# Attention's scores in one PSUM tile, scores and products tied in urgent chains

## The chip, the cores and the metric

The kernel runs on one core of a Trainium2 chip. The metric is the time of one execution in device microseconds; the time before is 1723.08 us, the median of three runs (1722.53 to 1729.99).

## The reference

Two request groups of 512 tokens with 1024 features pass through two layers with shared weights. Layer 0 is a bidirectional RWKV-7 time mixing with two scans; layer 1, which the change touches, is a neighbourhood attention over a grid of 8 rows x 64 columns with 16 heads of 64 features:

```python
proj = xn @ w_in + b_in
q, k, v, z = jnp.split(proj, 4, axis=-1)
...
s = jnp.einsum('bnqhd,bsnkhd->bhnqsk', qr, kr, preferred_element_type=f32)
s = jnp.where(mask, s + bias.astype(f32), NEG_INF)
p = jax.nn.softmax(s.reshape(s.shape[:4] + (-1,)), axis=-1).reshape(s.shape)
return jnp.einsum('bhnqsk,bsnkhd->bnqhd', p.astype(v.dtype), vr)
...
return (o.reshape(bsz, t, D_INNER) * jax.nn.silu(z)) @ w_o + b_o
```

Each token attends to a window of 8 rows x 16 columns. Norms stand before and after each layer.

## The kernel before, in words

Features lie on partitions, tokens on the free axis. A projection (`gemm`, L398 to L409) fills one PSUM bank of 128x512 with 24 matmuls: eight steps over the features, each as three matmuls of operands split in a high and a low part (L404 to L406). Its weights come by DMA through `raw`, are cast by ACT (L353, `whi`) and subtracted by DVE (L354, `wlo`).

The scan of layer 0 runs under an order written by hand. Behind it, `rest()` (L1655) opens new PSUM banks: two `pg` for projections, two `pt` for transposed probabilities, one `po` for attention's output, three `pm` for everything else. From here a scheduler orders each engine's queue: it takes the instruction with the lowest priority number among those that its own clock holds ready, and numbers run in program order. `high_priority(n)` lowers the numbers by n; `behind` (L263) makes one instruction stand behind another on one engine, without a semaphore. Engines then run their queues strictly in this order.

`rest()` weaves generators. The first request's last in-projections (`inproj`, L1298, four projections q, k, v, z for each pair of heads) and the out-projection of layer 0 (`out0`) are run with steps of attention (`heads`) between; then come the first request's output projection (`out1`, L1394), the norm in the second request (`norm0`, `rstds`: a sum by matmuls at L430, ACT and DVE, then a spread to all partitions by matmuls at L442), the second request's in-projections with its `heads`, transposes of the residual (`by_token`, L1421), and at last `last()` (L1427), the second request's output projection (L1463 to L1465). `inproj` evacuates on DVE (L1311) and ACT (L1315 to L1323) and stores q, k, v and z to DRAM (L306); `heads` loads them (L309).

`heads(s, p)` does a pair of heads. v is transposed by PE in two groups of four and three (L1342, in `pm`), copied by ACT to `vtok` (L1343). Then two rounds of two windows each follow. A round has four score matmuls (L1353), two windows n for each of two heads h; head 0 works on partitions 0 to 63, head 1 on 64 to 127, and each head has its `pm` tile. DVE adds the bias and takes the maximum (L1361), ACT takes the exponential (L1364), DVE divides (L1365, L1366), PE transposes two blocks for each score (L1368, in `pt`), and ACT copies them to `pts` (L1371). Eight product matmuls with v (L1381, two windows, two blocks e, two heads) add into `po`, with 64 output columns for each head. DVE multiplies `po` by the gate z (L1387). With 16 pairs of heads there are 32 rounds.

The words for matmul forms in the profile are rows*columns of the array: 128*128 for projections and transposes, 64*128 for scores, 128*64 for products. The prediction calls the latter two split forms, and one uninterrupted run of scores or of products on PE's queue a visit.

Of the kernel before, what the change touches and what calls it, by code (L numbers as in the profile page):

```python
# [13 lines left out]
ALU = mybir.AluOpType  # L14
# [4 lines left out]
P = 128  # L19
# [194 lines left out]
class Trunk:  # L214
    NACT, NW, NRAW, NXR, NTMP, WP = 18, 4, 3, 3, 5, 512
    POST0, POST, POST2, POST3, NPA = 0.7, 1.0, 0.15, 0.66, 5
    HP, HS = (1000, 0), 1000
    OUT1 = ("pg", "pg", "pm", "pm")
    LOW = 15
    LA = -40  # L220
    LATER = (0, 40, 0, 0)
    POST4 = 0.2
    LAST = ("pg", "pg", "pm", "pm")
    PG, PT, NK, NPT = 2, 2, 2, 3
# [1103 lines left out]
    def heads(self, s, p):  # L1328

        nc = self.nc  # L1330
        vt, act, gps = nc.vector, nc.scalar, nc.gpsimd
        a = lambda tag, shape=(P, T), n=1, dt=F32: self.t(tag, shape, n, dt, self.ap)
        bias = a("bias", (P, 2, 3, 256), self.NBI)
        for h in range(2):
            self.load(bias[:, h].rearrange("p a b -> p (a b)"), self.a["rpb"][2 * p + h])
        q, k, v = (self.load(a(kind, n=2), self.sp[kind, s, p]) for kind in ("q1", "k1", "v1"))
        yield
        vtok = a("vtok", (P, 7, P), self.NK)
# [6 lines left out]
        op = self.p("po", (P, 4, P))  # L1345
        cols = (0, 8, 24, 32)
        for ns in ((0, 1), (2, 3)):

            scs = [self.p("pm", (P, 2, 256)) for h in range(2)]
            for n in ns:  # L1350
                for h in range(2):
                    hs = slice(64 * h, 64 * h + 64)
                    nc.tensor.matmul(  # L1353
                        scs[h][:, n % 2], q[hs, n * P:(n + 1) * P], k[hs, 8 * cols[n]:8 * cols[n] + 256], start=True, stop=True)
            pts = []
            for n in ns:
                pt = self.p("pt", (P, 2, 2, P))
                for h in range(2):
                    sb = a("sb", (P, 256), self.NSB)
                    mx = a("mx", (P, 4), 6)  # L1360
                    vt.tensor_tensor_reduce(  # L1361
                        sb, scs[h][:, n % 2], bias[:, h, (0, 1, 1, 2)[n]], 1.0, -3.0e38, op0=ALU.add, op1=ALU.max, accum_out=mx[:, 0:1])
                    vt.tensor_scalar(mx[:, 1:2], mx[:, 0:1], -1.0, None, op0=ALU.mult)  # L1363
# [10 lines left out]
            if ns[1] == 3:  # L1374
                while ("z1", s, p) not in self.sp:
                    yield
                z = self.load(a("z1"), self.sp["z1", s, p])
            for n in ns:
                for e in range(2):
                    for h in range(2):  # L1380
                        nc.tensor.matmul(  # L1381
                            op[64 * h:64 * h + 64, n], vtok[:, cols[n] // 8 + 2 * e, 64 * h:64 * h + 64], pts[n % 2][:, h, e],
                            start=(e == 0), stop=(e == 1))
            yield
# [270 lines left out]
    def rest(self, prep, mid):  # L1655
        prep.close()
        mid.close()
        self.banks(self.stack, pg=self.PG, pt=self.PT, po=1, pm=7 - self.PG - self.PT)
        self.gt = "pg"
# [165 lines left out]
```

## Time and profile before

| what | us |
|---|---|
| median of three runs | 1723.08 |
| profiled execution, its own time | 1721.11 |
| its span, first to last instruction | 1719.3 |
| PE busy in the span | 1583.5 |
| DVE busy | 1246.5 |
| ACT busy | 982.9 |
| first matmul of `rest()` starts at | 1178.81 |

Read the page's slices first, to see in which part of the span an engine is full; then cut that part out in the table by windows; then read the timeline by start times. Matmuls overlap on PE, so the distance from one start to the next is what one costs, and the duration in its row is longer.

### The profile page before, as it was taken

Reading aid. Unit: us, or ns where it says so; the run is one execution under the profiler, and the core shown is the slowest. Engines: PE = TensorE matmul, PEld = TensorE weight load, DVE = VectorE, ACT = ScalarE, POOL = GpSimd, SP = SyncE. Lnnn points to the kernel's source line nnn. Section 1 sums busy time; section 2 is a strip of 40 time slices with the busy share of each in tenths; the row PEclk is TensorE's granted clock in tenths of the full one; section 3 lists DMA queues with packets and bytes.
Section 4 is the critical chain, followed back from the end, with each engine's and each line's share of the span. In section 5 each row is a group of like instructions: output and inputs, shape, how many; then the busy total and the mean of one; then the engine's idle time right before and its main releaser. Section 6 shows DMA issues by size and latency. Waiting matters only on the chain. (4 is left out here: it accounts for less than half of the span.)

```text
span 1719.3 us, 45887 instructions
## 1 busy us (share of the span) xinstructions
PE 1583.5 (92%) x18624; PEld 1209.3 (70%) x18624; DVE 1246.5 (73%) x2725; ACT 982.9 (57%) x1975; POOL 24.1 (1%) x94
## 2 busy tenths in 40 slices
PE   7999787999988999789988799999999999999998
PEld 6766555776766767567766677777777787777776
DVE  8986678788877867898788898655565586555474
ACT  5444655767755675656576545544556664555462
POOL 0000000000000000000000000000000000000000
PEclk9989999999999989899999799999999999999999
DMA  5435687786566678766587564547564248555553
GB/s 204 166 117 202 208 278 230 221 273 224 184 201 205 206 239 252 240 217 216 188 263 229 191 209 146 177 147 246 178 197 146 93 147 268 163 164 160 163 169 98
DMA packets 240819, 336.23 MB, mean 196 GB/s; under 512 B 53696, under 2 KB 119360, under 8 KB 240608
## 3 DMA queue, kind: packets, MB, share of 16 engines
q1 hardware_dynamic: 240608, 333.31, 60.4%
q8 instruction: 146, 2.39, 0.6%
q14 instruction: 65, 0.53, 0.1%
HBM read 227.71 MB, written 105.51 MB: 194 GB/s over the span
## 5 line engine op out<-in xcount | busy, mean ns | idle before, releaser
L747 PE MATMUL pm<-act,whi 128*128 128x512 f32 x608 | 272.9, 449 | 13.1 <-ACT whi L699 9.9
L749 PE MATMUL pm<-act,wlo 128*128 128x512 f32 x608 | 248.8, 409 | 18.2 <-DVE wlo L701 18.2
L748 PE MATMUL pm<-act,whi 128*128 128x512 f32 x608 | 248.9, 409 | 7.7 <-DVE act L727 6.1
L404 PE MATMUL pg<-act,whi 128*128 128x512 f32 x448 | 181.4, 406 | 0.0
L405 PE MATMUL pg<-act,whi 128*128 128x512 f32 x448 | 178.1, 398 | 0.0
L406 PE MATMUL pg<-act,wlo 128*128 128x512 f32 x448 | 178.0, 398 | 0.0
L353 ACT CAST whi<-raw 128x512 fp32r<-128x512 f32 x156 | 96.2, 617 | 142.6 <-PE pg L405 71.8
L354 DVE TENSOR_TENSOR wlo<-raw,whi 128x512 fp32r<-128x512 f32 x156 | 106.7, 686 | 73.9 <-ACT whi L353 56.9
L747 PEld LDWEIGHTS pm<-act,whi 128*128 128x128 f32 x608 | 119.3, 196 | 56.3 <-issue 13.9
L749 PEld LDWEIGHTS pm<-act,wlo 128*128 128x128 f32 x608 | 119.9, 197 | 52.1 <-DVE wlo L701 25.4
L748 PEld LDWEIGHTS pm<-act,whi 128*128 128x128 f32 x608 | 120.1, 198 | 30.5 <-DVE act L727 8.6
L701 DVE TENSOR_TENSOR wlo<-raw,whi 128x512 fp32r<-128x512 f32 x152 | 102.8, 683 | 33.3 <-ACT whi L699 32.6
L699 ACT CAST whi<-raw 128x512 fp32r<-128x512 f32 x152 | 92.7, 617 | 27.9 <-PE pm L748 11.1
L404 PEld LDWEIGHTS pg<-act,whi 128*128 128x128 f32 x448 | 84.2, 188 | 23.7 <-issue 8.8
L406 PEld LDWEIGHTS pg<-act,wlo 128*128 128x128 f32 x448 | 84.2, 188 | 18.9 <-issue 2.8
L405 PEld LDWEIGHTS pg<-act,whi 128*128 128x128 f32 x448 | 84.3, 188 | 17.8 <-issue 3.0
L938 DVE TENSOR_TENSOR N<-etmp,N 128x30 f32<-128x30 f32 (+14 forms) x240 | 79.8, 332 | 8.3
L1361 DVE CUSTOM_DVE_ANT_0 sb<-pm,bias 128x256 f32<-128x256 f32 x128 | 50.1, 420 | 47.3 <-PE pm L1353 36.1
L937 DVE TENSOR_TENSOR etmp<-N 128x30 f32<-128x30 f32 (+14 forms) x240 | 78.7, 328 | 4.8
L1364 ACT ACTIVATE sb<-sb,mx 128x256 f32<-128x256 f32 x128 | 64.1, 502 | 30.7 <-DVE mx L1363 30.5
L1022 PE MATMUL pf<-cab 64*64 64x128 f32 (+1 forms) x2048 | 72.4, 270 | 3.4 <-issue 2.4
L1045 DVE TENSOR_TENSOR AK<-zy,cc 128x256 f32<-128x256 f32 x63 | 26.6, 422 | 64.2 <-PE zy L1010 64.0
(363 smaller groups left out, 3379.1 us busy)
## 6 DMA issues: line engine op xcount, KB each, us to landing
dab<-ab SPq DMA_DIRECT2D x32, 1024.0 KB, 7.1
cab<-dab SPq DMA_DIRECT2D x64, 512.0 KB, 4.5
raw<-in_w_in_dram SPq DMA_DIRECT2D x128, 256.0 KB, 2.9
bias<-in_rpb_dram SPq DMA_DIRECT2D x32, 384.0 KB, 4.7
raw<-in_w_z_dram SPq DMA_DIRECT2D x32, 256.0 KB, 4.6
dz<-tmp SPq DMA_DIRECT2D x32, 256.0 KB, 2.2
raw<-in_w_k_dram SPq DMA_DIRECT2D x32, 256.0 KB, 2.5
dk<-tmp SPq DMA_DIRECT2D x32, 256.0 KB, 3.0
```

What stands on the lines that cost most here:

```text
L353: self.nc.scalar.copy(hi, src)
L354: (eng or self.nc.vector).tensor_tensor(lo, src, hi.bitcast(F32), op=ALU.subtract)
L404: nc.tensor.matmul(ps, hi, x[k][0], start=(k == 0), stop=False)
L405: nc.tensor.matmul(ps, hi, x[k][1], start=False, stop=False)
L406: nc.tensor.matmul(ps, lo, x[k][0], start=False, stop=(k == KT - 1))
L699: nc.scalar.copy(hi, raw[h])
L701: nc.vector.tensor_tensor(lo, raw.pop(h), hi.bitcast(F32), op=ALU.subtract)
L747: nc.tensor.matmul(ps, hi[:, at], xh, start=(k == 0), stop=False)
L748: nc.tensor.matmul(ps, hi[:, at], xl, start=False, stop=False)
L749: nc.tensor.matmul(ps, lo[:, at], xh, start=False, stop=(k == KT - 1))
L937: vt.tensor_tensor(tv, N[:, q + 1:, q:q + 1].broadcast_to([P, n, q]), N[:, q:q + 1, :q].broadcast_to([P, n, q]), op=ALU.mult)
L938: vt.tensor_tensor(N[:, q + 1:, :q], tv, N[:, q + 1:, :q], op=ALU.add)
```

## The change

The four scores of a round share one tile `sc` of two banks, a bank for each head, with one buffer; `pm` keeps one bank (the sum stays eight). The scores of a round get the priority 1000 ahead and each stands behind the one before, so that they come in the order window 0 head 0, window 0 head 1, window 1 head 0, window 1 head 1. The products with v get the same, with the round's second window first. `out1` takes `pg` for all eight projections; `last()` takes `po` for its third bank. Line numbers from 219 on are one higher in the changed kernel, from the scores on three to eleven higher.

```diff
--- before.py
+++ after.py
@@ -215,12 +215,13 @@
     NACT, NW, NRAW, NXR, NTMP, WP = 18, 4, 3, 3, 5, 512
     POST0, POST, POST2, POST3, NPA = 0.7, 1.0, 0.15, 0.66, 5
     HP, HS = (1000, 0), 1000
-    OUT1 = ("pg", "pg", "pm", "pm")
+    OUT1 = ("pg", "pg", "pg", "pg")
+    HPA = 1000
     LOW = 15
     LA = -40
     LATER = (0, 40, 0, 0)
     POST4 = 0.2
-    LAST = ("pg", "pg", "pm", "pm")
+    LAST = ("pg", "pg", "po", "pm")
     PG, PT, NK, NPT = 2, 2, 2, 3
     AHEAD, AHEADW, SCAN_A, SCAN_W = 0, 0, 300, 300
     NAB, NX, NR, NY, NSB, NBI = 2, 2, 2, 2, 4, 1
@@ -1346,12 +1347,17 @@
         cols = (0, 8, 24, 32)
         for ns in ((0, 1), (2, 3)):
 
-            scs = [self.p("pm", (P, 2, 256)) for h in range(2)]
-            for n in ns:
-                for h in range(2):
-                    hs = slice(64 * h, 64 * h + 64)
-                    nc.tensor.matmul(
-                        scs[h][:, n % 2], q[hs, n * P:(n + 1) * P], k[hs, 8 * cols[n]:8 * cols[n] + 256], start=True, stop=True)
+            scs = self.p("sc", (P, 2, 2, 256))
+            with self.tc.high_priority(self.HPA):
+                last = None
+                for n in ns:
+                    for h in range(2):
+                        hs = slice(64 * h, 64 * h + 64)
+                        one = nc.tensor.matmul(
+                            scs[:, h, n % 2], q[hs, n * P:(n + 1) * P], k[hs, 8 * cols[n]:8 * cols[n] + 256], start=True, stop=True)
+                        if last is not None:
+                            self.behind(one, last)
+                        last = one
             pts = []
             for n in ns:
                 pt = self.p("pt", (P, 2, 2, P))
@@ -1359,7 +1365,7 @@
                     sb = a("sb", (P, 256), self.NSB)
                     mx = a("mx", (P, 4), 6)
                     vt.tensor_tensor_reduce(
-                        sb, scs[h][:, n % 2], bias[:, h, (0, 1, 1, 2)[n]], 1.0, -3.0e38, op0=ALU.add, op1=ALU.max, accum_out=mx[:, 0:1])
+                        sb, scs[:, h, n % 2], bias[:, h, (0, 1, 1, 2)[n]], 1.0, -3.0e38, op0=ALU.add, op1=ALU.max, accum_out=mx[:, 0:1])
                     vt.tensor_scalar(mx[:, 1:2], mx[:, 0:1], -1.0, None, op0=ALU.mult)
                     act.activation(sb, sb, AF.Exp, bias=mx[:, 1:2], accum_out=mx[:, 2:3])
                     vt.reciprocal(mx[:, 3:4], mx[:, 2:3])
@@ -1375,12 +1381,17 @@
                 while ("z1", s, p) not in self.sp:
                     yield
                 z = self.load(a("z1"), self.sp["z1", s, p])
-            for n in ns:
-                for e in range(2):
-                    for h in range(2):
-                        nc.tensor.matmul(
-                            op[64 * h:64 * h + 64, n], vtok[:, cols[n] // 8 + 2 * e, 64 * h:64 * h + 64], pts[n % 2][:, h, e],
-                            start=(e == 0), stop=(e == 1))
+            with self.tc.high_priority(self.HPA):
+                last = None
+                for n in ns[::-1]:
+                    for e in range(2):
+                        for h in range(2):
+                            one = nc.tensor.matmul(
+                                op[64 * h:64 * h + 64, n], vtok[:, cols[n] // 8 + 2 * e, 64 * h:64 * h + 64], pts[n % 2][:, h, e],
+                                start=(e == 0), stop=(e == 1))
+                            if last is not None:
+                                self.behind(one, last)
+                            last = one
             yield
         with self.tc.high_priority(self.HP[s] if p == NP - 1 else 0):
             o = self.tmp() if s else self.t("oa", (P, T), NP, F32, self.ap)
@@ -1655,7 +1666,7 @@
     def rest(self, prep, mid):
         prep.close()
         mid.close()
-        self.banks(self.stack, pg=self.PG, pt=self.PT, po=1, pm=7 - self.PG - self.PT)
+        self.banks(self.stack, pg=self.PG, pt=self.PT, po=1, sc=1, pm=5 - self.PG - self.PT)
         self.gt = "pg"
         self.ap = self.pool(self.stack)
         queue = [self.heads(0, p) for p in range(self.NPA)]
```

The first place is on PE, at the first pair of heads (`sc`, and before `pm` from 16341 up, are scores; `pt` transposed probabilities; other `pm` with v are v's transposes; `pg` is a projection). Before, an x2 of one tile is two windows of one head:

```order
L404 MATMUL pg_16389<-act_13337,whi_16385 128x512
L1353 MATMUL pm_16342<-k_2857_16312,q_2856_16310 128x256 x2
L1353 MATMUL pm_16442<-k_2857_16312,q_2856_16310 128x256 x2
L405 MATMUL pg_16389<-act_13336,whi_16385 128x512
L406 MATMUL pg_16389<-act_13337,wlo_16386 128x512
L404 MATMUL pg_16487<-act_12216,whi_16479 128x512
L1368 MATMUL pt_16347<-cc,sb_16348 128x128 x2
L405 MATMUL pg_16487<-act_12215,whi_16479 128x512
L406 MATMUL pg_16487<-act_12216,wlo_16480 128x512
```

The same place in the change:

```order
L406 MATMUL pg_16391<-act_13336,whi_16387 128x512
L1343 MATMUL pm_16335<-cc,v_2859_16317 128x128 x2
L1356 MATMUL sc_16444<-k_2858_16315,q_2857_16313 128x256 x4
L1343 MATMUL pm_16335<-cc,v_2859_16317 128x128
L1374 MATMUL pt_16349<-cc,sb_16350 128x128 x2
L1374 MATMUL pt_16349<-cc,sb_16370 128x128 x2
L1374 MATMUL pt_16403<-cc,sb_16404 128x128 x2
L1374 MATMUL pt_16403<-cc,sb_16416 128x128 x2
L407 MATMUL pg_16391<-act_13337,wlo_16388 128x512
```

The second round's scores stood as head 0 beside the first round's head 1, and its head 1 came later; now the four are one row, and the first round's eight transposes stand together.

The second place is on PE too, at the second pair of heads, whose second round has the tiles 16706 and 16707:

```order
L406 MATMUL pg_16658<-act_12970,wlo_16655 128x512
L1353 MATMUL pm_16706<-k_2922_16573,q_2921_16571 128x256
L1353 MATMUL pm_16707<-k_2922_16573,q_2921_16571 128x256
L1368 MATMUL pt_16608<-cc,sb_16624 128x128 x2
L1368 MATMUL pt_16665<-cc,sb_16666 128x128 x2
L1353 MATMUL pm_16706<-k_2922_16573,q_2921_16571 128x256
L1368 MATMUL pt_16665<-cc,sb_16678 128x128 x2
L1353 MATMUL pm_16707<-k_2922_16573,q_2921_16571 128x256
L404 MATMUL pg_16658<-act_13286,whi_16654 128x512
```

In the change this round's scores are `sc_16706`, and `po_16343` is the first pair's output:

```order
L406 MATMUL pg_16565<-act_12560,whi_16561 128x512
L407 MATMUL pg_16565<-act_12561,wlo_16562 128x512
L1389 MATMUL po_16343<-pts_16528,vtok_16322 64x128 x4
L1389 MATMUL po_16343<-pts_16495,vtok_16322 64x128 x4
L1356 MATMUL sc_16706<-k_2921_16574,q_2920_16572 128x256 x4
L1343 MATMUL pm_16594<-cc,v_2922_16576 128x128 x3
L1374 MATMUL pt_16608<-cc,sb_16609 128x128 x2
L405 MATMUL pg_16565<-act_12970,whi_16561 128x512
L406 MATMUL pg_16565<-act_12969,whi_16561 128x512
```

Scores that stood in four rows among transposes are one row, directly behind the first pair's last eight products.

The third place is the last norm of the first request on PE (sum L430, spread L442). Before, the spread stands 18 projection matmuls behind the sum:

```order
L406 MATMUL pg_18861<-act_18747,wlo_18854 128x512
L430 MATMUL pm_18817<-ones,acc_3375_18320 128x1 x4
L404 MATMUL pg_18861<-act_18751,whi_18853 128x512
L405 MATMUL pg_18861<-act_18750,whi_18853 128x512
L406 MATMUL pg_18861<-act_18751,wlo_18854 128x512
L404 MATMUL pg_18861<-act_18755,whi_18853 128x512
```

In the change (sum L431, spread L443, with one `pm` bank):

```order
L406 MATMUL pg_18848<-act_18757,whi_18844 128x512
L407 MATMUL pg_18848<-act_18758,wlo_18845 128x512
L431 MATMUL pm_18804<-ones,acc_3360_18307 128x1 x4
L443 MATMUL pm_18817<-tmp_18812,ones 128x128 x4
L405 MATMUL pg_18913<-act_18730,whi_18905 128x512
L406 MATMUL pg_18913<-act_18729,whi_18905 128x512
```

The spread is now the sum's direct neighbour, and the next projection stands behind both.

## The prediction

> **What bounds the kernel now.** I read the page first: its slices for where in the span PE is full, then the chain that ended last.
>
> ```profile
> PE   7999787999988999789988799999999999999998
> ...
> PE 36%; DVE 4%; DMA 2%; ACT 2%; issue 1%; SPq 0%; DVEq 0%; ACTq 0%
> PE pg L404 6%; PE pg L405 6%; PE pg L406 6%; PE pm L1353 3%; PE po L1381 2%; PE pt L1368 2%; PE pm L747 2%; PE pm L748 1%; PE pm L749 1%; DMA raw<-in_w_ao_dram 1%; DMA raw<-in_w_in_dram 1%; PE pf L1022 1%; PE pm L1342 1%; PE us L1119 1%; PE zy L1093 0%
> ```
>
> The last slices are full on PE, and the chain runs mostly through PE: the projections (L404 to L406), then scores, products and transpositions of attention. All the edits lie in this last stage, from the first matmul of `rest()` to PE's last one. So I cut that stretch out in the table by windows, and asked what PE waited for there:
>
> ```profile
> 1178.80:1711.50 532.70, 529.75 (x2849) 408.38 (x2847) 316.76 (x971) 293.65 (x649) 0.00 (x0) 1.00 0.52 166
> ...
> PE pm L1342 <- DMA v<-dv: 2.2, 1, 2.2
> PE pm L1353 <- ACT vtok L1343: 0.4, 1, 0.4
> PE pg L1463 <- ACT os L353: 0.3, 1, 0.3
> ```
>
> The columns of the first row are length, PE, PEld, DVE, ACT. PE is busy 529.75 of 532.70 us and waits 2.9 us in all; DVE is busy 59%, ACT 55%. The granted clock is 1.00. The stage is as long as PE's queue of matmuls, so the change is worth what it does to that queue, less the waits it adds. "Busy" doesn't yet say that the array is used well: the start times do.
>
> **What an attention visit costs PE.** These rows of the timeline show start, time and form; a score or a product is listed as two matmuls, so x8 under L1353 is four scores, x4 two.
>
> ```profile
> 1196.25 0.39 PE L405 MATMUL pg<-act,whi 128*128 128x512 f32 x1
> 1196.47 0.39 PE L406 MATMUL pg<-act,wlo 128*128 128x512 f32 x1
> 1196.79 1.13 PE L1353 MATMUL pm<-k,q 64*128 64x256 f32 x4
> 1197.85 0.50 PE L404 MATMUL pg<-act,whi 128*128 128x512 f32 x1
> 1198.19 0.40 PE L405 MATMUL pg<-act,whi 128*128 128x512 f32 x1
> ...
> 1216.79 0.70 PE L1353 MATMUL pm<-k,q 64*128 64x256 f32 x4
> 1217.42 0.66 PE L1368 MATMUL pt<-cc,sb 128*128 128x128 f32 x4
> ...
> 1516.07 1.13 PE L1353 MATMUL pm<-k,q 64*128 64x256 f32 x8
> 1517.14 0.50 PE L404 MATMUL pg<-act,whi 128*128 128x512 f32 x1
> ...
> 1230.08 0.60 PE L1342 MATMUL pm<-cc,v 128*128 128x128 f32 x4
> 1230.43 0.48 PE L404 MATMUL pg<-act,whi 128*128 128x512 f32 x1
> 1230.84 0.66 PE L1381 MATMUL po<-pts,vtok 128*64 128x128 f32 x8
> 1231.43 0.50 PE L405 MATMUL pg<-act,whi 128*128 128x512 f32 x1
> ...
> 1212.10 1.09 PE L1381 MATMUL po<-pts,vtok 128*64 128x128 f32 x16
> 1213.12 0.50 PE L405 MATMUL pg<-act,whi 128*128 128x512 f32 x1
> ...
> 1274.55 0.66 PE L1381 MATMUL po<-pts,vtok 128*64 128x128 f32 x8
> 1275.14 0.66 PE L1368 MATMUL pt<-cc,sb 128*128 128x128 f32 x4
> 1275.55 0.48 PE L405 MATMUL pg<-act,whi 128*128 128x512 f32 x1
> ```
>
> Projection matmuls start 0.22 to 0.23 apart; I use 0.227. What follows from start to start:
> - Two scores of one head (at 1196.79; the order shows one tile) hold PE 1.06 us. Four scores, two of each head (1516.07), hold it 1.07. Two scores of different heads (1216.79) hold it 0.63. The heads run side by side; the price goes by the head with most scores: 0.63 for one, 1.06 for two, 0.43 more for each further.
> - Products of one window (1230.84) hold PE 0.59, of both windows of a round (1212.10) 1.02.
> - Entering such a split form takes 0.32 instead of 0.227 (1196.47 to 1196.79): 0.09 more. Leaving it to projections takes 0.34 for the first (1197.85 to 1198.19): 0.11 more. Leaving to transpositions takes 0.06 more: 0.41 for four after a product (1275.14) against 0.35 after a projection (1230.08).
>
> **The change, part by part.** Only the order and the waits change; all matmuls stay. I counted the visits in both orders on PE, from the first score to the end.
>
> *Scores in one tile, tied.* Before: 56 visits, 44 with two scores on the fuller head, 11 with one, 1 with three: 44 x 1.06 + 11 x 0.63 + 1.49 = 55.1 us. After: 39 visits, 30 with two and 9 with one: 37.5 us. Saved 17.6. In 25 of 32 rounds the four stand together; in the other seven the equally urgent products cut in, and that is in the count.
>
> *Products tied.* Before: 26 rounds whole, ten half visits, one round cut into a first piece and the rest (about 1.4): 26.5 + 5.9 + 1.4 = 33.8. After: 32 x 1.02 = 32.6. Saved 1.2. The reversed order of the windows costs nothing by itself: both products are ready when the later one is.
>
> *Fewer changes of form.* Products and scores now stand side by side more often (27 direct neighbours against 6), so PE enters a split form 44 times instead of 88. Entering: 88 x 0.09 + 55 exits to projections x 0.11 + 33 to others x 0.06 = 16.0; after, 44 x 0.09 + 30 x 0.11 + 14 x 0.06 = 8.1. Saved 7.9. Transpositions go the other way, from 102 visits to 123: 0.01 each (0.35 to the next projection, then 0.32 for it, against four times 0.109 and 0.227), about 0.2 lost.
>
> Sum on PE's queue: 17.6 + 1.2 + 7.9 - 0.2 = **26.5 us less**.
>
> *One bank for transposes.* `pm` falls from three banks to one, so each use now waits for the evacuation of the last. In the changed order three neighbours stand too close for that.
>
> ```profile
> 1417.21 0.95 PE L430 MATMUL pm<-ones,acc 128*128 128x1 f32 x8
> ...
> 1418.71 0.88 DVE L438 TENSOR_SCALAR tmp<-cc,rs 128x128 f32<-128x128 f32 x4
> ...
> 1422.42 0.60 PE L1421 MATMUL pm<-cc,hh 128*128 128x128 f32 x4
> ...
> 1423.06 0.58 ACT L1423 COPY tmp<-pm 128x512 f32<-128x512 f32 x1 [0.27 <-PE pm L1421]
> ...
> L1371 ACT COPY pts<-pt x64: 563/586/595, 1200.6 to 1679.6; 128x512 f32<-128x512 f32 x64
> ```
>
> The last norm of the first request gets its sum (L430) and its spread (L442) as neighbours. In the rows the sum's eight matmuls end at about 1418.0, and DVE has the spread's operand at 1418.71 + 0.88 = 1419.6: PE would wait 1.6 us. In the present order 18 projection matmuls cover that; the cover is gone. Two pairs of transposition groups follow each other: from the last one's start (about 1422.75) to the copy's end at 1423.64 is 0.9, so 0.8 each. At one place a product stands 0.6 us behind the start of its last transposition; that takes 0.3 and the copy to `pts` 0.59, so some 0.4 more. Together 3.6 us, with the whole queue behind, as PE is in order. Bounds: nothing, if the groups have drifted apart, to 6, if each copy waits for another of its length.
>
> *One score tile.* A round's first score now waits until all four reductions of the last round have read the tile; before, it had a bank free. The trace shows how long that takes, at its quickest and its slowest:
>
> ```profile
> 1303.47 1.13 PE L1353 MATMUL pm<-k,q 64*128 64x256 f32 x8
> ...
> 1304.64 0.42 DVE L1361 CUSTOM_DVE_ANT_0 sb<-pm,bias 128x256 f32<-128x256 f32 x1 [2.10 <-PE pm L1353]
> ...
> 1305.74 0.42 DVE L1361 CUSTOM_DVE_ANT_0 sb<-pm,bias 128x256 f32<-128x256 f32 x1
> ...
> 1667.21 1.13 PE L1353 MATMUL pm<-k,q 64*128 64x256 f32 x4
> ...
> 1673.35 0.42 DVE L1361 CUSTOM_DVE_ANT_0 sb<-pm,bias 128x256 f32<-128x256 f32 x1
> ```
>
> From the visit's start to the end of the fourth read are 2.7 us (1303.47 to 1306.16), in the last round of all 6.6 (1667.21 to 1673.77). In the changed order the nearest next visit starts its own 1.07, 22 projection matmuls and four transpositions later: 6.7 us. So I take nothing. The other end is an estimate: were each round 1.6 us slower than this slowest, at 8.2, the 15 rounds that stand closer than that would lose 12 us together; that is a rival below. A gain is excluded, as no bank is added.
>
> *Output projections in `pg`, the last stage's `po`.* The nearest two users of one `pg` bank stand 2.1 us apart, twice the 0.9 of the `pm` turn above; `po` is first used after the last head's products. Nothing, to 2 us at the end, if the weights for the last stage come late.
>
> Added waits together about 4 us; net **22 us less**. The profiled execution took 1721.11 us for its span of 1719.3; less 22 it is 1699. The median of the runs shown is 2 us higher: **1701 us**.
>
> **A page against it.** In the rows, evacuation of a round's scores takes DVE four reads of about 0.35 from start to start, 1.5 us, while PE writes them in 1.07. The Trainium skill, page "TensorEngine Tiling (Array Packing)", section "PSUM Bottleneck", warns that packing speeds up TensorE but not the evacuation of PSUM, so that the copy out may become the bottleneck. By that rule the gain would end at the reads; by the rows, DVE has 41% of the stage free.
>
> **The rivals.**
> - *The score tile's readers set the pace.* For it: one tile instead of three banks, and PE asks earlier. Against it: 2.7 to 6.6 us of reading under a distance of 6.7 and more. At the 12 us above given back: 1713.
> - *The load of k sets the pace, and the kernel gets slower.* Urgent scores now stand nearer to the projection that makes their k: 39 projection matmuls, eight products and eight transpositions, 11.1 us, for six heads of the second request; before it was over 21. If the load isn't there, all of PE's queue stands behind the scores.
>
> ```profile
> 1515.53 0.39 PE L406 MATMUL pg<-act,wlo 128*128 128x512 f32 x1
> ...
> 1517.66 0.42 SPq L306 DMA_DIRECT2D dk<-tmp  x1
> ...
> 1520.78 0.33 SPq L309 DMA_DIRECT2D k<-dk  x1
> ...
> k<-dk SPq DMA_DIRECT2D x6, 256.0 KB, 3.7
> ```
>
>   From that projection's end (1515.9) over the store to the load's landing (1520.8 + 3.7) are 8.6 us: 2.5 to spare. It costs from 11.1 us on, for each of six heads; to lose all 22 and 9 more, the load would have to land 16.3 us after, twice as late. SP's order around these loads hardly moves. At that price: 1732.
> - *The path isn't PE's queue after all, or the waits move to DVE and ACT*: within 5 us of before, 1719. Against it: 2.9 us of waits in 533.
>
> **How the numbers follow.** Forecast 0.80 (1701, on its own 1694 to 1708), readers 0.10, no change 0.06, k load 0.04. The low end is the queue's full 26.5 and 2 us of the present waits gone too: 1694. The high end takes in the readers' case: 1713. A measurement of this kernel can tell about 0.5%, 8.6 us, from no change, so below 1714.5 is faster: 0.87 with most of the readers' case; within 0.09; slower 0.04.
>
> **What would show it.** In the changed profile the stretch from the first `pg` matmul to PE's last should be about 510 us, PE still over 98% busy; the scores' line should fall from the busy time in the row below to about 41 (37.5 and the tails of 39 visits, some 0.07 each); PE's waits should name the norm's spread and the transposes behind ACT copies, some 4 us. The reads of the score tile in that list at over 5 us would make the first rival right, a DMA of k the second. The stage up to 1178.8 keeps its order and its time; a change there would be none of these.
>
> ```profile
> L1353 PE MATMUL pm<-k,q 64*128 64x256 f32 x256 | 59.3, 405 | 0.4 <-ACT vtok L1343 0.4
> ```

## The result and the profile after

The changed kernel takes **1707.18 us** (median of four runs, 1700.71 to 1711.44) against 1723.46 us for the kernel before on the same chip (four runs, 1722.53 to 1729.99). The ratio is 0.9887 with a 95% interval from 0.9863 to 0.9911: faster by 1.1%. The forecast was 1701, in a range of 1694 to 1713.

The profiled execution of the changed kernel took 1709.09 us, 12.0 less than the one before. I split both at the same two instructions, the first `pg` matmul of `rest()` and PE's last matmul. The stage between them fell from 532.7 to 511.8 us, 20.9 less, where the prediction had 22. The scan ahead of it rose from 1178.8 to 1187.7 us, although each engine runs the same instructions in the same order there (15776 matmul records on PE, 972 transfers issued by SP, in both).

First the stage. These are the table by windows for the changed kernel, the group of its scores, and the list of PE's waits in the stage; the columns are those of the rows shown of before.

```profile
1187.60:1699.50 511.90, 506.12 (x2849) 399.52 (x2848) 316.17 (x971) 292.77 (x649) 0.00 (x0) 1.00 0.55 174
...
L1356 PE MATMUL sc<-k,q 64*128 64x256 f32 x256 | 40.3, 406 | 1.6 <-DMA k<-dk 1.6
...
PE sc L1356 <- DMA k<-dk: 1.6, 2, 1.3
PE pg L405 <- DVE tmp L1312: 1.2, 1, 1.2
PE pm L443 <- DVE tmp L439: 1.0, 1, 1.0
PE pm L1474 <- ACT vtok L1344: 1.0, 1, 1.0
PE pm L1432 <- ACT tmp L1434: 0.7, 1, 0.7
PE pm L1432 <- ACT vtok L1344: 0.3, 1, 0.3
```

PE is still busy 98.9% of a shorter stage (506.12 of 511.90), so the stage is still the length of PE's queue. The scores' line is busy 40.3 us instead of 59.3; about 41 was forecast. The waits sum to 5.8 us against 2.9, and no line names the readers of the score tile. Three lines were priced at nothing: k's load, a projection behind DVE's evacuation of a `pg` bank (L1312), and the last stage's `pm` bank behind ACT's copy of v (L1474).

The timeline shows how scores now stand. The first three rows are a round whose four scores are together, the others one of the seven rounds into which the products cut.

```profile
1499.74 0.40 PE L407 MATMUL pg<-act,wlo 128*128 128x512 f32 x1
1500.07 1.13 PE L1356 MATMUL sc<-k,q 64*128 64x256 f32 x8
1501.13 0.50 PE L405 MATMUL pg<-act,whi 128*128 128x512 f32 x1
...
1521.70 0.70 PE L1356 MATMUL sc<-k,q 64*128 64x256 f32 x2 [0.39 <-DMA k<-dk]
1522.32 1.09 PE L1389 MATMUL po<-pts,vtok 128*64 128x128 f32 x16
1523.35 1.13 PE L1356 MATMUL sc<-k,q 64*128 64x256 f32 x6
1524.40 0.50 PE L405 MATMUL pg<-act,whi 128*128 128x512 f32 x1
```

The whole round holds PE 1.06 us (1500.07 to 1501.13), the cut one 0.62 and 1.05. Scores and products that stand side by side are one entry into a split form instead of two.

Next the scan. This is the granted clock in the page's forty slices, first of the kernel before, then of the changed one.

```profile
PEclk9989999999999989899999799999999999999999
```

```profile
PEclk9989888899999999889999799999999999999999
```

Counted from 1, the slices 5 to 8 and 18 show a lower clock in the changed kernel's run, slice 15 a higher one, all ahead of the stage (which begins in slice 28). Half-speed time within the scan is 139.9 us against 122.9, by the trace's rows of the clock. If PE sets the pace there, half of that is lost: 8.5 of the 8.9 us. That this explains the scan is not shown: in the run `again` below, the same kernel has as long a scan (1187.6 us) with 129.7 us at half speed, and half of its 6.8 us more is only 3.4.

### The profile page after: what moved, and what is told of

It reads as the page before. It is cut to its first block, busy times and chain, and to the rows that moved or that the text cites. A ratio compares the mean times of both kernels' runs of the same rounds, so it can differ in the third digit from the quotient of the medians.

```text
span 1707.3 us, 45868 instructions
## 1 busy us (share of the span) xinstructions
PE 1568.7 (92%) x18624; PEld 1207.7 (71%) x18624; DVE 1246.4 (73%) x2725; ACT 982.3 (58%) x1975; POOL 24.1 (1%) x94
## 4 chain that ended last, share of the span: by engine, by line
PE 64%; DVE 17%; DMA 8%; ACT 7%; issue 4%; SPq 1%; DVEq 0%; ACTq 0%
PE pg L405 6%; PE pg L406 6%; PE pg L407 6%; PE pm L748 6%; PE pm L750 4%; PE pm L749 4%; PE pf L1023 3%; PE sc L1356 2%; PE us L1120 2%; PE us L1134 2%; DVE etmp L938 2%; PE zy L1094 2%; DVE wlo L702 2%; PE po L1389 2%; DVE N L939 2%
## 5 line engine op out<-in xcount | busy, mean ns | idle before, releaser
L748 PE MATMUL pm<-act,whi 128*128 128x512 f32 x608 | 276.3, 454 | 13.3 <-ACT whi L700 9.7
L749 PE MATMUL pm<-act,whi 128*128 128x512 f32 x608 | 251.2, 413 | 8.1 <-DVE act L728 5.7
L405 PE MATMUL pg<-act,whi 128*128 128x512 f32 x480 | 198.5, 414 | 1.2 <-DVE tmp L1312 1.2
L406 PE MATMUL pg<-act,whi 128*128 128x512 f32 x480 | 190.7, 397 | 0.0
L407 PE MATMUL pg<-act,wlo 128*128 128x512 f32 x480 | 189.9, 396 | 0.0
L748 PEld LDWEIGHTS pm<-act,whi 128*128 128x128 f32 x608 | 120.8, 199 | 56.8 <-issue 13.0
L749 PEld LDWEIGHTS pm<-act,whi 128*128 128x128 f32 x608 | 122.1, 201 | 31.4 <-DVE act L728 8.3
L700 ACT CAST whi<-raw 128x512 fp32r<-128x512 f32 x152 | 92.7, 617 | 29.4 <-PE pm L749 13.8
L405 PEld LDWEIGHTS pg<-act,whi 128*128 128x128 f32 x480 | 90.8, 189 | 20.9 <-issue 4.2
L407 PEld LDWEIGHTS pg<-act,wlo 128*128 128x128 f32 x480 | 90.8, 189 | 19.3 <-issue 0.3
L406 PEld LDWEIGHTS pg<-act,whi 128*128 128x128 f32 x480 | 90.9, 189 | 18.0 <-issue 3.5
L1367 DVE CUSTOM_DVE_ANT_0 sb<-sc,bias 128x256 f32<-128x256 f32 x128 | 50.2, 420 | 37.1 <-PE pt L1374 31.7
```

What stands on the lines that cost most here:

```text
L405: nc.tensor.matmul(ps, hi, x[k][0], start=(k == 0), stop=False)
L406: nc.tensor.matmul(ps, hi, x[k][1], start=False, stop=False)
L407: nc.tensor.matmul(ps, lo, x[k][0], start=False, stop=(k == KT - 1))
L748: nc.tensor.matmul(ps, hi[:, at], xh, start=(k == 0), stop=False)
L749: nc.tensor.matmul(ps, hi[:, at], xl, start=False, stop=False)
```

## The experiments

All stage lengths are cut at the same two instructions. "Scan" is the time up to the stage, in the profiled execution.

| label | time, us | scan | stage |
|---|---|---|---|
| before | 1721.11, profiled run | 1178.8 | 532.7 |
| after | 1709.09, profiled run | 1187.7 | 511.8 |
| again | 1709.64, median of 6 | 1187.6 | 512.6 |
| banks_alone | 1710.82, one run | 1182.3 | 519.2 |
| ties_alone | 1712.54, one run | 1183.1 | 519.9 |
| scores_only | 1716.62, one run | 1187.4 | 520.0 |
| products_only | 1706.67, one run | 1176.9 | 520.6 |
| no_urgency | 1722.28, one run | 1192.0 | 521.0 |
| by_head | 1707.16, one run | 1185.1 | 512.4 |
| bias_later | 1710.48, one run | 1188.4 | 512.6 |
| bias_behind | 1705.85, one run | 1185.0 | 511.6 |
| fenced_bias | 1699.74, median of 6 | 1184.2 | 506.9 |
| fenced | 1693.61, median of 4 | 1180.7 | 505.3 |
| before_2 | 1717.01, one run | 1174.1 | 533.2 |

The total misleads here: `products_only` ran 2.4 us quicker than the profiled run of after while its stage is 8.8 us longer. So the stages are compared.

**The same kernel again.** The changed kernel without an edit.

> The changed kernel once more. Queue theory (the last stage is as long as PE's queue of matmuls, and that queue is what it was): the stretch from the first pg matmul to PE's last takes 512 us again, within 1. The scan before it has the same order in both kernels. If its 1187.7 us, against 1178.8 of before, were chance in the granted clock, it lies anywhere from 1177 to 1191 now, and the total differs from before by 21 us plus or minus 8. If the denser last stage caused it, it is over 1185 again and the ratio stays near 0.990.

The median of six runs is 1709.64 us (1703.75 to 1712.27) against 1727.12 (11 runs), a ratio of 0.9895 with an interval from 0.9872 to 0.9919. The stage is 512.6, so the two profiles of this kernel agree to 0.8 us, and the gain is no accident of one run. The scan took 1187.6 us, which lies over 1185 and also inside the 1177 to 1191 for chance, so this run doesn't tell the two theories of the scan apart. Two things differ from the first profile within the same order: PE's waits (5.0 us in all) hold none for k, and 6.8 us instead of 3.4 run at half speed.

**The new banks without the ties.** One score tile and the new banks on the kernel before, with the bank choices of `out1` and `last()` that go with them; scores and products in the loops of before.

```diff
-            scs = [self.p("pm", (P, 2, 256)) for h in range(2)]
+            scs = self.p("sc", (P, 2, 2, 256))
...
-        self.banks(self.stack, pg=self.PG, pt=self.PT, po=1, pm=7 - self.PG - self.PT)
+        self.banks(self.stack, pg=self.PG, pt=self.PT, po=1, sc=1, pm=5 - self.PG - self.PT)
```

> One score tile and the new banks, but no ties and no urgency. Queue theory, by the visits in its order (42 of scores: 29 with two on the fuller head, 13 with one; products 26 whole and 12 half; 79 entries into split forms): 18.7 us less than before, so the last stage takes 514 us plus the waits for the single pm bank, 514 to 518. The theory that the ties and the urgency bring the gain: 530 to 535, as before or a little worse.

**The ties without the new banks.** Chains and urgency as changed, two `pm` tiles for a round's scores, banks as before.

```diff
-            scs = self.p("sc", (P, 2, 2, 256))
+            scs = [self.p("pm", (P, 2, 256)) for h in range(2)]
```

> Ties and urgency with the banks and the two score tiles of before. Queue theory (51 visits of scores, 32 with two on the fuller head and 19 with one; products all whole; 79 entries): 12.5 us less than before, so the last stage takes 520 us, and none of the waits for the single pm bank. The theory that the ties and the urgency bring the gain: 512, as the whole change.

The table by windows for the two stages, `banks_alone` first:

```profile
1182.30:1701.45 519.15, 513.57 (x2849) 399.29 (x2847) 315.25 (x971) 294.42 (x649) 0.00 (x0) 1.00 0.54 172
...
L1354 PE MATMUL sc<-k,q 64*128 64x256 f32 x256 | 41.9, 407 | 0.3 <-DMA k<-dk 0.3
```

```profile
1183.06:1702.92 519.86, 516.92 (x2849) 401.72 (x2847) 315.43 (x971) 293.44 (x649) 0.00 (x0) 1.00 0.53 170
...
L1356 PE MATMUL pm<-k,q 64*128 64x256 f32 x256 | 49.8, 410 | 0.4 <-ACT vtok L1344 0.4
```

Either half brings most of the gain: 13.5 us for the banks, 12.8 for the ties, 20.9 for both. In `banks_alone` the scores' line falls to 41.9 us with no tie at all: 22 of 32 rounds stand whole, against 9 before. The likely reason is that one tile has one moment at which it is free, so the four scores become ready at once and the scheduler puts them in a row. With two tiles, tied scores still stand in 51 visits. `banks_alone` came out 1.2 us above what was expected and `ties_alone` met it.

**Scores tied, products not.** The loop of the products as before (its windows in the old order too).

```diff
-            with self.tc.high_priority(self.HPA):
-                last = None
-                for n in ns[::-1]:
+            for n in ns:
...
-                            if last is not None:
-                                self.behind(one, last)
```

> As the change, but products neither tied nor urgent. Queue theory: all 32 rounds of scores in one visit (33.9 us, less than the change's 37.5), but products fall apart into 64 pieces (38.3 us against 32.7) and PE enters split forms 72 times; 18.8 us less than before, so 514 to 517 for the last stage. The theory that only the scores matter: 512 or less.

The stage is 520.0, so both theories' numbers are missed, and the direction is that of the first. These are the products in the timeline and in the groups of this kernel.

```profile
1514.63 0.66 PE L1387 MATMUL po<-pts,vtok 128*64 128x128 f32 x8
1515.22 0.50 PE L405 MATMUL pg<-act,whi 128*128 128x512 f32 x1
...
L1387 PE MATMUL po<-pts,vtok 128*64 128x128 f32 x512 | 43.2, 287 | 1.8 <-ACT pts L1377 1.8
```

Each window's products stand alone, 64 visits instead of 32, at 0.59 us each. The scores are whole in all 32 rounds (34.1 us, less than in the change, since no product cuts in), but products take 6.0 us more and PE enters a split form 72 times instead of 44. The tie and the urgency of the products, which this run takes away together and the prediction priced at 1.2 us, protect far more once the scores are urgent.

**Products tied, scores not.** The reverse.

```diff
-            with self.tc.high_priority(self.HPA):
-                last = None
-                for n in ns:
-                    for h in range(2):
+            for n in ns:
+                for h in range(2):
...
-                        if last is not None:
-                            self.behind(one, last)
```

> The changed kernel with the scores neither tied nor urgent; products stay tied and urgent, banks as changed. By the count the scores take 44 visits (39.8 us for 37.5), PE enters a split form 72 times instead of 44 (12.4 us for 8.1), products as changed: 6.2 us more than the change, so 518 us; the other variants with many changes of form came out 3 to 5 us above their count, so up to 522. If one tile for the four scores already brings them together and their ties are idle, the stage is 512 to 513 us.

The stage is 520.6, inside the 518 to 522 of the count. The tie and the urgency of the scores aren't idle beside the one tile: without them the scores take 44 visits and PE enters a split form 72 times.

**Ties without urgency.**

```diff
-    HPA = 1000
+    HPA = 0
```

> As the change, but the urgency is 0: ties and tile stay. Queue theory: 44 visits of scores (28 with two, 16 with one), 74 entries into split forms; 19.4 us less than before, so the last stage takes 513 to 516 us. A theory that the gain comes from scores being early (attention's chain on DVE and ACT starts sooner): about 530.

The stage is 521.0, which is 5 us above the count's 513 to 516 and far below the 530 of the theory that being early is what gains. Without urgency the chains stand among the other work again: 44 visits of scores for 39, and 74 entries for 44. The table by windows and the waits of this kernel:

```profile
1192.04:1713.03 520.99, 514.43 (x2849) 401.40 (x2847) 314.95 (x971) 292.70 (x649) 0.00 (x0) 0.99 0.53 171
...
PE pg L1474 <- DVE tmp L1312: 2.2, 1, 2.2
PE pm L1432 <- ACT tmp L1434: 1.8, 3, 0.7
PE pm L443 <- DVE tmp L439: 1.0, 1, 1.0
```

**What the stage is made of.** For every kernel I added up, from its trace: the scores' visits and the products' visits from start to start (without a wait directly behind one), the changes of form at the prediction's prices, the waits of the list, and half of the half-speed time. What is left of the stage should be the same work everywhere.

| label | scores (visits) | products (visits) | form changes (entries) | waits | half speed | left |
|---|---|---|---|---|---|---|
| before | 55.4 (56) | 33.9 (38) | 15.9 (88) | 2.9 | 0 | 424.6 |
| before_2 | 55.9 (56) | 34.1 (38) | 15.9 (88) | 2.8 | 0 | 424.5 |
| banks_alone | 39.0 (42) | 33.8 (38) | 13.8 (79) | 5.6 | 1.7 | 425.2 |
| ties_alone | 46.2 (51) | 32.8 (32) | 13.7 (79) | 2.9 | 0 | 424.3 |
| scores_only | 34.1 (32) | 38.8 (64) | 13.4 (72) | 6.3 | 1.7 | 425.6 |
| products_only | 39.9 (44) | 32.9 (32) | 12.4 (72) | 6.6 | 3.4 | 425.5 |
| no_urgency | 40.2 (44) | 33.4 (34) | 12.7 (74) | 6.5 | 3.4 | 424.9 |
| after | 37.6 (39) | 32.8 (32) | 8.1 (44) | 5.8 | 1.7 | 425.8 |
| again | 37.6 (39) | 33.1 (32) | 8.1 (44) | 5.0 | 3.4 | 425.4 |
| by_head | 39.5 (39) | 32.8 (32) | 8.1 (44) | 6.0 | 0 | 426.0 |
| bias_later | 38.4 (41) | 32.8 (32) | 8.2 (44) | 6.9 | 0 | 426.3 |
| bias_behind | 38.4 (41) | 32.8 (32) | 8.1 (44) | 5.8 | 0 | 426.5 |
| fenced_bias | 34.1 (32) | 32.9 (32) | 8.2 (44) | 3.9 | 1.7 | 426.1 |
| fenced | 34.1 (32) | 32.8 (32) | 8.1 (44) | 3.1 | 1.7 | 425.5 |

The rest lies between 424.3 and 426.5 us while the stages differ by 28. So the five columns, four of them measured in each kernel, account for every stage to within 1.1 us of the middle. The expectations that were missed by a few us had summed visits and entries and allowed at most 4 us for waits and half-speed time; those two make up 10 us in `no_urgency` and 8 in `scores_only`, against 3 in `ties_alone`, which met its number. The price of a change of form enters as forecast and wasn't measured by itself, and the rest shows that it is somewhat too high: with 44 entries it is 425.4 and more, with 79 and 88 at most 425.2. A straight line through the fourteen stages less the other four columns gives 0.14 us for each entry with its exit, where the prices come to 0.17 to 0.19. By this estimate the 44 saved entries are worth about 6 us, not 7.9.

**Scores by head instead of by window.** The chain's order is head 0 twice, then head 1 twice.

```diff
-                for n in ns:
-                    for h in range(2):
+                for h in range(2):
+                    for n in ns:
```

> As the change, but the tie runs through both windows of head 0 and then both of head 1. If the two heads run side by side on PE whatever their order, a visit of four still holds PE 1.07 us and the last stage takes 513 us, 1 to 2 more than the change, for five visits that are cut worse. If heads must alternate to overlap, a visit holds PE 1.9 us and the stage takes 535 or more.

The stage is 512.4, and a round's four scores hold PE just as long:

```profile
1226.01 1.14 PE L1356 MATMUL sc<-k,q 64*128 64x256 f32 x8
1227.08 0.50 PE L405 MATMUL pg<-act,whi 128*128 128x512 f32 x1
```

That is 1.07 us. The prediction's price, which goes by the fuller head and not by the order, holds. The 1.9 us more in its scores' column belong to the cut rounds: a cut in the middle leaves two scores of one head on either side, not one of each, so 34 visits instead of 30 have two on the fuller head (4 x 0.43 = 1.7).

**The load of k.** In the changed kernel PE waits for k at two of the eight pairs, which the prediction had at 2.5 us to spare. SP's queue shows why, here of the changed kernel (the first row issues both bias loads of the pair, 768 KB):

```profile
1571.43 0.90 SPq L310 DMA_DIRECT2D bias<-in_rpb_dram  x2
1572.38 0.49 SPq L310 DMA_DIRECT2D raw<-in_w_in_dram  x1
1572.97 0.37 SPq L307 DMA_DIRECT2D dk<-tmp  x1
1580.27 0.33 SPq L310 DMA_DIRECT2D k<-dk  x1
```

From the issue of the store of k to the issue of its load pass 7.3 us; for the pair in the prediction's rows it was 3.1 (1517.66 to 1520.78), with the bias loads behind the store. The first try moved the bias load behind those of q, k and v in `heads`:

```diff
-        for h in range(2):
-            self.load(bias[:, h].rearrange("p a b -> p (a b)"), self.a["rpb"][2 * p + h])
         q, k, v = (self.load(a(kind, n=2), self.sp[kind, s, p]) for kind in ("q1", "k1", "v1"))
+        for h in range(2):
+            self.load(bias[:, h].rearrange("p a b -> p (a b)"), self.a["rpb"][2 * p + h])
```

> As the change, but a pair of heads loads its bias behind q, k and v instead of ahead of them. If the bias loads slow the store of k that stands behind them (from its issue to the issue of the load of k 6 to 7 us in the changed profile, 2 to 3 before), PE's waits for k go from 4.1 us to nothing and the store takes about 3 us again; the last stage takes 509 to 511. If they don't, the waits stay and the stage takes 512.

The stage is 512.6, and the expectation is missed because the edit didn't do what it was for: the scheduler, which takes what is ready, still issued the bias 1.5 us ahead of the store, and PE waited 2.0 us for k. (The 4.1 us in the expectation are PE's 1.6 and 2.5 of its weight loads, which overlap.) The second try ties them on SP's queue:

```diff
+        got = [nc.sync.dma_start(x, self.sp[kind, s, p]) for kind, x in (("q1", q), ("k1", k), ("v1", v))]
         for h in range(2):
-            self.load(bias[:, h].rearrange("p a b -> p (a b)"), self.a["rpb"][2 * p + h])
+            one = nc.sync.dma_start(bias[:, h].rearrange("p a b -> p (a b)"), self.a["rpb"][2 * p + h])
+            self.behind(one, got[1])
```

> The changed kernel with the two bias loads of a pair ordered behind its load of k on SP's queue (moving them in the code had left SP's order as it was). If the bias loads ahead of the store of k are what makes it slow, the time from the store's issue to the issue of k's load falls from 6 to 7 us to the 2 to 3.5 us of the kernel before, and the waits of scores for k (1.6 to 2.0 us) go; by the count of visits PE's queue is 0.9 us longer (41 visits of scores for 39), so the stage comes to about 511 us. If other traffic makes the store slow, store to load stays at 6 to 7 us, the waits stay, and the stage is 513 us or more.

SP's queue for the same pair, and PE's waits:

```profile
1570.34 0.33 SPq L307 DMA_DIRECT2D dk<-tmp  x1
1573.51 0.33 SPq L1336 DMA_DIRECT2D k<-dk  x1
1573.89 0.89 SPq L1338 DMA_DIRECT2D bias<-in_rpb_dram  x2
...
PE po L1391 <- ACT sb L1372: 1.8, 1, 1.8
PE pg L405 <- DVE tmp L1312: 1.3, 2, 1.2
PE pm L443 <- DVE tmp L439: 1.0, 1, 1.0
PE pm L1434 <- ACT tmp L1436: 0.7, 1, 0.7
PE sc L1358 <- DMA k<-dk: 0.6, 1, 0.6
```

Store to load is now 3.2 us, 2.2 to 3.8 at the last six pairs: at these pairs the bias loads ahead of the store are what made it slow. They aren't the only thing that can: at the second request's first pair, with no bias load near the store, it took 6.0 us in the changed kernel and still takes 5.7. The wait for k is 0.6 us against 1.6, but that fall shows little, since `again`, with store to load at 3.7 to 6.4 us at these pairs, had no such wait at all. And the stage is 511.6, no better: products now wait 1.8 us for probabilities, and two more visits of scores cost 0.8 us. That the later bias makes the probabilities late fits the row, but wasn't tried by itself.

**A fence for the scores.** The seven cut rounds have one origin, urgent scores that stand too early, and the waits for k may have the same. So the first score of a round goes behind the products of the round before last (for a pair's first round in the second request, of the last round). This ran first together with the edit of `bias_later`:

```diff
+                        elif len(self.done_v) > 1:
+                            self.behind(one, self.done_v[-1 if s and ns[0] == 0 else -2])
...
+            self.done_v.append(last)
...
+        self.done_v = []
```

> The bias later, and each round's first score behind the last product of the round before last (in the second request, at the start of a pair of heads, of the last round), so that products can't cut into scores. Queue theory: 32 visits of scores, all whole, 33.9 us against 37.5: 3.3 us less than the change on PE's queue, and the waits for k gone: 506 to 509 for the last stage. A theory that the change has reached what this stage can give: 511 to 513.

The median is 1699.74 us, a ratio to before of 0.9864 (0.9834 to 0.9893); the stage is 506.9, at the expected number. To see which edit did it, the fence ran alone:

> The changed kernel with one edit: the first score of a round stands behind the products of the round before last (for a pair's first round: of the last round). The bias load is where the change has it. If the fence by itself makes the earlier best version, the stage goes by the count: 32 visits of scores with two on the fuller head are 33.9 us against 37.5, so 3.6 less than the change's 511.8 to 512.6, and the two waits for k (1.6 to 2.0 us) go too, since scores stand further from their k: 506 to 508 us. If the bias load's place in the code had a share, this comes out at 509 or above, with the waits for k still there.

Its stage, its scores and its waits:

```profile
1180.73:1686.07 505.34, 502.22 (x2849) 397.63 (x2847) 315.39 (x971) 293.15 (x649) 0.00 (x0) 1.00 0.54 177
...
L1356 PE MATMUL sc<-k,q 64*128 64x256 f32 x256 | 36.3, 402 | 0.9 <-DMA k<-dk 0.9
...
PE pm L443 <- DVE tmp L439: 1.0, 1, 1.0
PE sc L1356 <- DMA k<-dk: 0.9, 1, 0.9
PE pm L1435 <- ACT tmp L1437: 0.7, 1, 0.7
```

The stage is 505.3, below the expected 506 to 508, with the bias where the change has it: the fence is the whole of it. All rounds are whole (32 visits, 34.1 us, 3.5 less than in the change), and the waits are 3.1 us against 5.8 and, in `again`, 5.0. The wait for k didn't go, as was expected (0.9 us): the fence cures the cut rounds, and for k's load it shows nothing. The median of `fenced`, **1693.61 us** (1691.59 to 1700.59), is the best here: 0.9832 of before, with an interval from 0.9799 to 0.9866.

**The kernel before once more**, for the scan.

> The kernel before once more, unchanged, for the scan ahead of the stage, which the change doesn't touch. If the 8.9 us by which the changed kernel's scan was longer come from the granted clock alone, this scan lies anywhere between 1178.8 and 1192 us, with its half-speed time to match; if the change itself makes the scan longer, it is at 1180 us or below again. The stage, whose order is the same, should repeat its 532.7 us to within 1 us in either case, plus half of any half-speed time granted in it.

The stage repeats to 0.5 us (533.2). The scan is 1174.1 us: that is the second theory's 1180 or below, not the first's 1178.8 to 1192. It is also 4.7 us shorter than the other scan of the same kernel, with 10.3 us less half-speed time (112.6 for 122.9), so the scan varies by itself. Of the twelve scans of changed kernels only `products_only` (1176.9) lies below the longer of the two; their mean is 1185.0. Whether the change lengthens the scan by some 4 us is left open: the medians, 16.3 and 17.5 us apart where the stages are 20 to 21 apart, speak for it, as do those of `fenced_bias` (23.0 and 25.8 to 26.3); those of `fenced`, 30.0 apart where the stages are 27.3 to 27.9 apart, speak against it, and so does the spread of 1176.9 to 1192.0 with one and the same order. Nor does the half-speed time settle it: over the fourteen scans it goes with their length (0.45 us for each us, correlation 0.86), but a scan less half of its half-speed time still lies anywhere from 1114.2 (`fenced`) to 1122.8 (`again`).

## Why the prediction was right, step by step

The changed kernel's time lies inside the range, 6 us above 1701. The mechanism was the right one: the stage is PE's queue, and scores that stand together make it shorter. That the total fits is in part luck: 1707.18 is just inside the forecast's own 1694 to 1708, and the median of `again`, 1709.64, is inside only the part up to 1713 that was added for slow readers, which weren't the reason.

- *Scores*: 17.6 forecast, 17.8 measured (55.4 to 37.6). *Products*: 1.2 forecast, 1.1 measured. The prices read from six places of the timeline of before held.
- *Changes of form*: 88 and 44 entries were counted and are there; 7.9 is their price by the prediction. With it and the other terms the remainders of the two kernels are 424.6 and 425.8, so 1.2 us are not accounted for. By the line through all fourteen kernels that is mostly this term, sized at 7.9 where about 6 is likelier.
- *Added waits*: net 4 forecast, 2.9 measured, but the items differ. The norm's spread cost 1.0 for 1.6, one of the two `pm` turns 0.7 and the other 0.3 for 0.8 each, the product behind its copy nothing for 0.4. The terms put at nothing brought 1.6 (k's load), 1.2 (a `pg` bank not yet evacuated) and 1.0 (the last stage), inside their bounds of 2 where one was given. And the 2.9 us of before went. The errors cancelled, by luck. In `again` the same order brought 5.0 us with other items, so single waits repeat only in part.
- *One score tile*: nothing forecast, nothing measured. The rule of the Trainium skill, page "TensorEngine Tiling (Array Packing)", section "PSUM Bottleneck", would have ended the gain at the readers; the trace shows no such limit, as no wait names them.
- *The rivals*: that of the readers didn't happen. That of k's load happened at two of eight pairs in one profile and at none in the other, and cost 1.6 us and nothing, not 31. The working there took the store as quick as in the quoted rows (3.1 us) and found that SP's order hardly moved; the one move that counted, the bias loads ahead of the store, was missed: the rows were read for k alone. The rival of no change didn't happen: the stage fell by 20 to 21 us in both profiles.
- *The step that failed* is in the last paragraph: "The stage up to 1178.8 keeps its order and its time". Its order stayed, its time was 8.9 us longer in the profiled run. That alone lifts the profiled 1699 by 8.9, and the stage's missing 1.1 makes it 1709. The base was one profiled run, and the prediction carried no term for how much the scan varies. Why it was longer stays open.

A term of the stage was missing as well: where waits stood close together, a stretch at half speed followed. This is the place, in the timeline of the changed kernel just behind the last norm of the first request, and the same stretch in the table by windows.

```profile
1423.59 0.60 PE L1432 MATMUL pm<-cc,h 128*128 128x128 f32 x4
1424.87 0.66 PE L1432 MATMUL pm<-cc,hh 128*128 128x128 f32 x4 [0.68 <-ACT tmp L1434]
1426.67 0.49 PE L405 MATMUL pg<-act,whi 128*128 128x512 f32 x1 [1.16 <-DVE tmp L1312]
...
1428.21 0.63 PE L407 MATMUL pg<-act,wlo 128*128 128x512 f32 x1
1428.63 0.63 PE L405 MATMUL pg<-act,whi 128*128 128x512 f32 x1
...
1424.20:1427.60 3.40, 1.58 (x8) 1.22 (x9) 3.02 (x6) 1.50 (x4) 0.00 (x0) 1.00 0.73 225
1427.60:1431.02 3.42, 3.42 (x10) 2.64 (x9) 1.29 (x2) 1.03 (x3) 0.00 (x0) 0.50 0.99 320
1431.02:1450.00 18.98, 18.98 (x100) 14.82 (x99) 11.71 (x36) 10.61 (x22) 0.00 (x0) 1.00 0.95 330
```

Two waits fall into one stretch in which PE is busy 1.58 of 3.40 us; in the next 3.42 the granted clock is 0.50 and projections start 0.42 apart instead of 0.23. That stretch does 1.7 us less work, more than either wait cost. In `by_head` the same two waits (0.7 and 1.2 us) stand at the same place and no half-speed stretch follows; the last section has the likely reason.

## What to carry to other kernels

Where two kinds of matmul share an engine's queue, count the visits and the changes of form in the two orders and price them from start to start. The ranges given from such counts ahead of the runs held or were missed by at most 5 us, and most of what they missed were waits and half-speed time. Making instructions urgent and tying them isn't enough: say also how early they may stand, or they cut other chains; a fence of a few lines was worth 5 to 7 us of the stage here. And before a profiled run is used as the base of a sum, ask which parts of it vary by themselves, since the part whose order a change leaves alone took from 1174.1 to 1192.0 us here, and 4.7 us apart in two runs of one kernel.

## What the hardware showed that was not expected

**The clock's slices.** In every profiled execution all half-speed stretches between its first microseconds and PE's last matmul begin on one grid of 3.413 us, to 1 ns, whose phase differs from run to run (the span began between 0.1 and 3.3 us into a slice). I cut all executions into these slices, took those that ran at full speed, and sorted them by PE's busy time in the slice:

| PE busy in the slice, us of 3.41 | slices | next one at half speed |
|---|---|---|
| below 1.4 | 165 | 165 |
| 1.4 to 1.6 | 67 | 61 |
| 1.6 to 1.8 | 72 | 30 |
| 1.8 to 2.0 | 68 | 19 |
| 2.0 to 2.6 | 326 | 26 |
| above 2.6 | 5615 | 0 |

So it takes no idle slice: after one in which PE was busy less than 1.4 us (41%) half speed always followed, after one above 2.6 us (76%) never, and between them the busy time alone doesn't decide. The Trainium skill, page "TensorE: Matmul & The Clock Gate", section "Part 1: The HAM clock gate", tells of a window of about 3.4 us that runs free of the kernel and of half speed after an idle window. The traces agree on the length and on the half speed, not on the idle: the slice shown in the changed kernel was busy 46%. Where a slice's edge falls among the waits thus changes what they cost: in the changed kernel the two waits left one slice at 1.58 us, and a half-speed slice, worth 1.7 us, followed; in `by_head` the poorest slice at that place was busy 1.98 us, and full speed followed. The scan, where PE waits often, took 1174.1 and 1178.8 us in one kernel and order; that the phase makes this difference is argued from the table and not shown, as the phase can't be chosen.

**A store behind loads.** Where the first bias load of a pair was issued 1.5 to 1.9 us ahead of the store of k on the same queue (23 stores in six profiles), the issue of k's load came 5.5 to 7.9 us behind that store. In `bias_behind`, with the bias loads behind k's load, it was 2.2 to 3.8 us at the last six pairs. The second request's first pair, with no bias load near the store, took 5.4 to 6.0 us in all kernels with one `pm` bank, which stays unexplained.
